# A decoder trunk's mixer: the tokens' factor folded into C and the convolved block, and some VectorE work pinned to a later place

## The chip, the cores and the metric

One core of a Trainium2 chip runs the whole program. The metric is the device time of one execution in microseconds (us); the times shown are medians of three runs. The profile comes from one further execution under the hardware profiler. Five engines work side by side, each in its own order: TensorE (PE, matmuls; PEld its weight loads), VectorE (DVE), ScalarE (ACT), GpSimd (POOL) and SyncE (SP). SP and GpSimd issue the transfers (DMAs) that are named here.

## The reference

Two layers of a decoder over 512 tokens of width 1024, everything float32. Each layer is a SwiGLU block, a mixer and another SwiGLU block. The mixer normalises, projects to q, k, v and three convolution parts, and joins attention and convolution by `w_out`:

```python
def short_conv(b_gate, c_gate, h_conv, conv_w):
    u = c_gate * h_conv
    ...
    y = lax.conv_general_dilated(
        u, w, window_strides=(1,), padding=[(CONV_K - 1, 0)],
        dimension_numbers=("NWC", "WIO", "NWC"), feature_group_count=CONV_WIDTH)
    return b_gate * y
...
        h = rms_norm(x, mix_norm[l])
        z = h @ w_in[l]
        ...
        attn_out = sliding_window_attention(q, k, v, attn_sink[l])
        conv_out = short_conv(z[..., V_END:CB_END], z[..., CB_END:CC_END],
                              z[..., CC_END:CH_END], conv_w[l])
        x = x + jnp.concatenate([attn_out, conv_out], axis=-1) @ w_out[l]
```

`rms_norm` divides each token by the root of its mean square and multiplies by a gain per feature. The convolution has three taps along the tokens and one filter for each of 512 features.

## The kernel before

Data lies transposed: features on the 128 partitions, the 512 tokens along the free axis. The norm's gain is put into the projection's input; the factor per token, `norm.inv` (the same value on all partitions, 128x512), is multiplied in after the matmul.

**Split numbers.** A float32 product is made of three matmuls in a rounded type: each matrix is split into a high part and the rest (`split`, L197: a copy on ScalarE, L198, and a subtraction on VectorE, L199). For weights the parts are the tiles `wh` and `wl`, three buffers of each. `split_far` (L201) makes the rest with a copy on ScalarE and an adding transfer that GpSimd issues (L205), and takes no VectorE time.

**Weights.** `plan` lists the 512 KB units in the order of use. `need_raw` gives a unit one of eight `raw` buffers and issues its load on SP (L182); a unit that is a sum of two blocks gets the second block by an adding transfer from GpSimd (L193). `need_split(g)` makes all splits up to number g, asking for loads LOAD_AHEAD = 4 units further. `take_split` (L257) hands out the split of the next matmul group, after `need_split` for SPLIT_AHEAD = 2 groups further.

**The mixer** (`mix`, L1149) of a layer has 18 groups of 24 matmuls (`group`, L263), each 128 columns of `w_in` by all tokens, into a PSUM tile `acc` (four buffers): k, v, four of q, and then for two pairs of feature blocks two of C, two of h and two of B. `scaled` (L1155) multiplies `acc` by `norm.inv` on VectorE into an SBUF tile: `cc`, `ch`, `cb`. From these: u = ch·cc (L1302, GpSimd), the three taps (L1304 and L1306 on ScalarE, L1307 on VectorE, L1310 on GpSimd) give y in the tile cc, and cb·y goes into `mixed[1]` (L1317, GpSimd; the last of the layer on VectorE).

Between these groups the attention runs in eight units (`Unit`), each with the stages `scores`, `turn` and `values`; `attend(step)` runs those that are due after the group of that step. `turn` transposes the probabilities p on TensorE into `pt` and splits them: `ph` on ScalarE, `pl` on VectorE (L1249). `values` then multiplies with the values into `o` (L1259 with ph, L1260 with pl).

**The output projection** uses a scheme with seven products of half-size blocks instead of eight (`Seven`, `share`). Its seven steps (`CHAINS`) multiply the blocks b11, b21, t2, t3, t1, t4, b22 of `mixed` (sums and differences of quarters) with the weights a11, a12, s2, s3, s1, a22, s4 of `w_out`, each weight in two halves h = 0 and 1. The accumulators are called x_m, w_m and y_m. s2 is the sum a11 + s1, made on VectorE in the raw buffers (L223). The blocks are split like weights: fb11h and fb11l, ft2h and ft2l and so on; t1, t4 and b22 are of the `far` kind. `soon` (L1323) says behind which step blocks are made early, in front of the additions into x (L747). Of a11, the first half is split by `split_far` in the `w_out` plan (L381).

**What sets the order.** A scheduler places the instructions of each engine when the program is built, by program order and by when it thinks their inputs ready; the waits of an engine are then in that fixed order. `tc.issue_after(ins)` adds one rule to it: what is recorded inside the block on the engine of `ins` comes behind `ins` on that engine. It adds no wait for `ins` to finish.

Of the kernel before, what the change touches and what calls it, by code (L numbers as in the profile page):

```python
# [1 line left out]

# [46 lines left out]
SPLIT_AHEAD = 2  # L49
# [9 lines left out]
def trunk_kernel(  # L59
# [23 lines left out]
    nc = tc.nc  # L83
# [11 lines left out]
    def g2(name, dt=F32, shape=(P, S)):  # L95
        return work.tile(list(shape), dt, tag="g2", bufs=14, name=name)
# [18 lines left out]
    def f32(ap):  # L115
        return ap.bitcast(F32)
# [50 lines left out]
    units = []  # L167
    order = []
    raw_of, split_of = {}, {}
    state = {"raw": 0, "split": 0, "group": 0}  # L170

    def add_unit(*unit):
        units.append(unit)
# [33 lines left out]
    def need_split(g):  # L207
        while state["split"] <= min(g, len(order) - 1):
            n = state["split"]
            u, what = order[n]  # L210
            far = what == "far"
            if what in (None, "wide", "far"):
                need_raw(u if far else u + LOAD_AHEAD)
                raw = raw_of.pop(u)
            elif isinstance(what, tuple):

                what, h, how = what
                far = how == "far"
                last = {"a11": 0, "a12": 4, "s2": 2, "s3": 6, "s1": 2, "a22": 8, "s4": 4}[what]
                need_raw(u + max(last, 4) + h + (0 if far else LOAD_AHEAD))  # L220
                a11, s1, a12, s3, a22 = (raw_of.get(u + 2 * i + h) for i in range(5))
                if what == "s2":
                    nc.vector.tensor_add(a11, a11, s1)  # L223
                raw = {"a11": a11, "a12": a12, "s2": a11, "s3": s3, "s1": s1, "a22": a22, "s4": a12}[what]
            else:

                need_raw(u + 4 + LOAD_AHEAD)
                a11, a12, s1, s3, a22 = (raw_of.get(u + i) for i in range(5))
                if what == "s2":
                    nc.vector.tensor_add(a11, a11, s1)  # L230
                if what == "s4":
                    nc.vector.tensor_add(a11, a11, a12)
                raw = {"a11": a11, "a12": a12, "s2": a11, "s3": s3, "s1": s1, "a22": a22, "s4": a11}[what]
                if what == FORMS[-1]:
                    for i in range(5):
                        del raw_of[u + i]
            shape = list(raw.shape)
            hi = wpool.tile(shape, F32R, tag="wh", bufs=3, name=f"wh_{n}")
            lo = wpool.tile(shape, F32R, tag="wl", bufs=3, name=f"wl_{n}")
            if far:  # L240
                split_far(hi, lo, raw)
            elif n:
                split(hi, lo, raw)
            if isinstance(order[n][1], tuple):
                if what == "s3" and how == "share":
                    nc.gpsimd.dma_start(out=a12, in_=a11, accum_op=ALU.add)
                elif what == "s3":
                    nc.vector.tensor_add(a12, a12, a11)
                done = {"s3": (0, 3), "s1": (1,), "a22": (4,), "s4": (2,)}.get(what, ())
                for i in done:  # L250
                    del raw_of[u + 2 * i + h]
            split_of[n] = (hi, lo)
            state["split"] += 1
            if far:
                need_raw(u + LOAD_AHEAD + (4 + h if isinstance(order[n][1], tuple) else 0))

    def take_split():  # L257
        n = state["group"]
        state["group"] += 1
        need_split(n + SPLIT_AHEAD if n else 0)  # L260
        return n, *split_of.pop(n)

    def group(rhs, between=None, own=None, order=range(KC)):  # L263
# [52 lines left out]
    def plan():  # L316
# [57 lines left out]
        for l in range(DEPTH):  # L374
            ffn(ffn1_wg[l], ffn1_wu[l], ffn1_wd[l], INNER if l else FIRST)
            for c in MIX_COLS:
                for j in range(2):
                    order.append((add_unit((w_in[l], 0, KC, (2 * c + j) * P, P)), None))
            seven(
                lambda o, j, h: (w_out[l], KC // 2 * j + 2 * h, 2, o * S, S),  # L380
                lambda what, h: "far" if (what, h) == ("a11", 0) else "share",  # L381
            )
            ffn(ffn2_wg[l], ffn2_wu[l], ffn2_wd[l], INNER if l + 1 < DEPTH else LAST)

# [168 lines left out]
    norm = Norm(0)  # L553
# [166 lines left out]
    def share(ops, by, between, y=None, soon=None):  # L720


        accs = {}
        for step, (acc, operand, start) in enumerate(CHAINS):
            ops.make(operand)
            xh, xl = ops.forms[operand]
            if start:
                tag = {"x": "mm", "y": "sc", "w": "aux"}[acc]
                shape = [P, 2, H] if y is None else [P, S]
                accs[acc] = [psum(tag, shape, f"{acc}_{ops.name}_{m}") for m in range(2)]  # L730
            o, t, sign = SHARES[step]
            for h in range(2):
                _, wh, wl = take_split()
                if y is None:
                    stand(accs[acc], wh, wl, xh, xl, h, start)
                else:
                    stream(accs[acc], wh, wl, xh, xl, h, start)
                if h == 0:
                    continue
                if soon:  # L740
                    ops.make(*soon.get(step, ()))
                for m in range(2):
                    if y is None:
                        part = xpair[2 * o + m][:, :, t * H : (t + 1) * H]
                    else:
                        part = y[2 * t + m][o]
                    nc.vector.scalar_tensor_tensor(  # L747
                        part, accs[acc][m], by * sign, part, op0=ALU.mult, op1=ALU.add
                    )
            if not soon and step < 3:  # L750
                ops.make(CHAINS[step + 4][1])
            between(step)
# [396 lines left out]
    def mix(l, norm, after):  # L1149
# [40 lines left out]
        class Unit:  # L1190
# [47 lines left out]
                    nc.vector.tensor_scalar(p, p, sums[:, h : h + 1], None, op0=ALU.mult)  # L1238

            def turn(self):  # L1240
                self.pt = []
                for kb in range(self.lo // P, 2):
                    tp = psum("aux", [P, 4, P], f"pt_{self.name}_{kb}")
                    for h in range(4):
                        nc.tensor.transpose(tp[:, h, :], self.p[:, h, kb * P : (kb + 1) * P], ident)
                    hi = g2(f"ph_{self.name}_{kb}", F32R, (P, 4, P))
                    lo = g2(f"pl_{self.name}_{kb}", F32R, (P, 4, P))
                    nc.scalar.copy(hi, tp)
                    nc.vector.tensor_sub(lo, tp, f32(hi))  # L1249
                    self.pt.append((kb, hi, lo))  # L1250

            def values(self):
                n, g = self.n, self.g
# [16 lines left out]

        def attend(step):

            for at, stage in ((VALUES_AT, "values"), (TURN_AT, "turn"), (SCORES_AT, "scores")):
                if step in at:
                    getattr(todo[at.index(step)], stage)()

        for j in range(NH // 2):
            acc = group(norm.h) if j else qacc
# [9 lines left out]
            q[2 * j], q[2 * j + 1] = qe, qo  # L1288
            attend(2 + j)

        step = 6
        for pair in range(2):
            cs = []
            for j in range(2):
                cs.append(scaled(group(norm.h), f"cc_{l}_{pair}_{j}"))
                attend(step)
                step += 1
            ys = []
            for j in range(2):
                c = 2 * pair + j  # L1300
                u = scaled(group(norm.h), f"ch_{l}_{pair}_{j}")
                nc.gpsimd.tensor_mul(u, u, cs[j])  # L1302
                y = cs[j]
                nc.scalar.activation(y, u, AF.Copy, scale=conv_of(l, 2, c))  # L1304
                tap = g2(f"tap_{l}_{c}")
                nc.scalar.activation(tap[:, 1:], u[:, : S - 1], AF.Copy, scale=conv_of(l, 1, c))  # L1306
                nc.vector.scalar_tensor_tensor(  # L1307
                    tap[:, 2:], u[:, : S - 2], conv_of(l, 0, c), tap[:, 2:], op0=ALU.mult, op1=ALU.add
                )
                nc.gpsimd.tensor_add(y[:, 1:], y[:, 1:], tap[:, 1:])  # L1310
                ys.append(y)
                attend(step)
                step += 1
            for j in range(2):
                b = scaled(group(norm.h), f"cb_{l}_{pair}_{j}")
                eng = nc.vector if pair and j else nc.gpsimd
                eng.tensor_mul(mixed[1][:, 2 * pair + j, :], b, ys[j])  # L1317
                attend(step)
                step += 1
                if step == 17:  # L1320
                    ops.make("b11")
        ops.make("b21", "b22")
        share(ops, 1.0, after.step, soon={0: ("t2", "t1"), 1: ("t3", "t4")})  # L1323

    class into:

# [53 lines left out]
```

## Time and profile before

| | us |
|---|---|
| median of three runs | 1692.35 (1691.88 to 1692.66) |
| the profiled execution's own time | 1690.47 |
| its span, first to last instruction | 1688.6 |
| mixer of layer one, first q group to the last `w_out` step | about 360 to 511 |
| the same in layer two | about 1194 to 1346 |
| granted TensorE clock, share of full | 0.999 |

The page of the profile gives each engine's busy time, then the chain of work that ended last, then groups of instructions by line. The waits view lists who waited for whom: total us, number of waits, the longest. The timeline gives start, duration, engine, line, operation, out<-in and shapes; the bracket behind a row is the idle time of the engine before it and who ended it. A 128x1024 operation of VectorE is listed with 1.22 us, but such operations follow each other at 1.14, since the end of one overlaps the start of the next. The same holds for 128x512 operations (0.69 listed, 0.60 apart) and for TensorE's matmuls (128x512: 0.39 listed, 0.23 apart; 128x256: 0.28 and 0.12).

### The profile page before, as it was taken

What the parts mean: (1) busy time and instruction counts of PE and PEld (TensorE: products, weight loads), DVE (VectorE), ACT (ScalarE), POOL (GpSimd) and SP (SyncE); (2) the same over time, 40 slices, a digit from 0 to 9 for tenths busy, and PEclk for the clock granted to TensorE, in tenths of its full rate; (3) what the DMA queues carried; (4) which work ended last, traced back from release to release, by engine and by line L of the source; (5) the groups of instructions that cost most, each with busy time, mean ns of one, the idle gap of its engine ahead of it and who ended that gap; (6) DMA issues with size and microseconds to landing.
All of it is one profiled execution on the core that took longest, in us unless ns stands there. A gap on an engine that the chain in (4) does not pass through costs nothing.

```text
span 1688.6 us, 23567 instructions
## 1 busy us (share of the span) xinstructions
PE 1675.1 (99%) x9014; PEld 1443.3 (85%) x9014; DVE 1382.8 (82%) x1817; ACT 967.7 (57%) x1335; POOL 215.3 (13%) x192
## 2 busy tenths in 40 slices
PE   9999999999999999999999999999999999999998
PEld 6888889988898888889988888999888988888886
DVE  7987679988799967799798677997787997667995
ACT  6545565466566655564465555644555766556654
POOL 1011111001221111111011111110013111111111
PEclk9999999999999999999999999999999999999999
DMA  8467787731597677778466777785226867777881
GB/s 250 104 171 189 186 199 187 188 100 51 135 215 167 174 183 186 187 191 221 150 144 179 187 186 183 198 202 156 63 63 143 219 137 195 184 183 185 224 213 51
DMA packets 191846, 284.19 MB, mean 168 GB/s; under 512 B 9004, under 2 KB 77684, under 8 KB 191732
## 3 DMA queue, kind: packets, MB, share of 16 engines
q1 hardware_dynamic: 151108, 199.95, 37.7%
q0 software_dynamic: 39472, 81.27, 28.6%
q8 instruction: 71, 1.16, 0.3%
q10 hardware_dynamic: 1152, 1.45, 0.2%
q14 instruction: 43, 0.35, 0.1%
HBM read 261.14 MB, written 2.10 MB: 156 GB/s over the span
## 4 chain that ended last, share of the span: by engine, by line
PE 93%; DVE 3%; DMA 2%; issue 1%; POOL 0%; ACT 0%; SPq 0%; ACTq 0%; POOLq 0%; DVEq 0%
PE x L711 25%; PE y L711 12%; PE x_s L696 8%; PE acc L273 7%; PE acc L276 7%; PE acc L280 7%; PE w L711 6%; PE y_s L696 4%; PE x_s L711 3%; PE w_s L696 2%; PE x_m L696 2%; PE at L917 2%; PE y_m L696 1%; PE y_s L711 1%; DMA wl<-raw 1%
## 5 line engine op out<-in xcount | busy, mean ns | idle before, releaser
L198 ACT CAST wh<-raw 128x1024 fp32r<-128x1024 f32 (+1 forms) x482 | 505.2, 1048 | 531.0 <-PE x L711 132.0
L199 DVE TENSOR_TENSOR wl<-raw,wh 128x1024 fp32r<-128x1024 f32 (+1 forms) x481 | 588.4, 1225 | 210.3 <-ACT wh L198 208.3
L273 PE MATMUL acc<-xh,wh 128*128 128x512 f32 x448 | 176.5, 394 | 0.1
L276 PE MATMUL acc<-xl,wh 128*128 128x512 f32 x448 | 175.5, 392 | 0.1
L280 PE MATMUL acc<-xh,wl 128*128 128x512 f32 x416 | 162.5, 391 | 0.0
L193 POOL DMA_DIRECT2D raw<-in_ffn_wu_dram x39 | 47.3, 1217 | 531.6 <-DMA raw<-in_ffn_wu_dram 306.8
L276 PEld LDWEIGHTS acc<-xl,wh 128*128 128x128 f32 x448 | 84.2, 188 | 18.5 <-DVE xl L421 1.7
L273 PEld LDWEIGHTS acc<-xh,wh 128*128 128x128 f32 x448 | 84.2, 188 | 17.1 <-issue 0.5
L280 PEld LDWEIGHTS acc<-xh,wl 128*128 128x128 f32 x416 | 78.1, 188 | 16.2
L193 POOL DMA_DIRECT2D raw<-in_ffn_wg_dram x39 | 47.2, 1249 | 228.0 <-DMA raw<-in_ffn_wu_dram 100.0
L223 DVE TENSOR_TENSOR raw<-raw,raw 128x1024 f32<-128x1024 f32 x58 | 70.9, 1229 | 6.3 <-DMA wl<-raw 5.7
L193 POOL DMA_DIRECT2D raw<-in_ffn_wd_dram x32 | 38.6, 1206 | 260.6 <-DMA raw<-in_ffn_wd_dram 142.4
L711 PE MATMUL w<-wh,fb21h 128*128 128x512 f32 x152 | 60.7, 399 | 0.0
L711 PE MATMUL x<-wh,ft2h 128*128 128x512 f32 x152 | 60.6, 398 | 0.0
L711 PE MATMUL y<-wh,ft3h 128*128 128x512 f32 x152 | 60.4, 398 | 0.0
L711 PE MATMUL w<-wl,fb21h 128*128 128x512 f32 x152 | 59.4, 391 | 0.0
L711 PE MATMUL x<-wl,ft2h 128*128 128x512 f32 x152 | 59.3, 390 | 0.0
L711 PE MATMUL y<-wh,ft3l 128*128 128x512 f32 x152 | 59.2, 390 | 0.0
L711 PE MATMUL y<-wl,ft3h 128*128 128x512 f32 x152 | 59.2, 390 | 0.0
L711 PE MATMUL w<-wh,fb21l 128*128 128x512 f32 x152 | 59.2, 389 | 0.0
L711 PE MATMUL x<-wl,fb11h 128*128 128x512 f32 x152 | 59.2, 389 | 0.0
L711 PE MATMUL x<-wh,fb11h 128*128 128x512 f32 x152 | 59.1, 389 | 0.0
(503 smaller groups left out, 4805.0 us busy)
## 6 DMA issues: line engine op xcount, KB each, us to landing
raw<-in_ffn_wu_dram SPq DMA_DIRECT2D x127, 512.0 KB, 4.3
raw<-in_ffn_wd_dram SPq DMA_DIRECT2D x104, 512.0 KB, 5.0
raw<-in_ffn_wg_dram SPq DMA_DIRECT2D x87, 512.0 KB, 5.0
raw<-in_ffn_wu_dram POOLq DMA_DIRECT2D x39, 512.0 KB, 8.0
raw<-in_ffn_wg_dram POOLq DMA_DIRECT2D x39, 512.0 KB, 6.0
raw<-in_w_in_dram SPq DMA_DIRECT2D x36, 512.0 KB, 3.6
raw<-in_ffn_wd_dram POOLq DMA_DIRECT2D x32, 512.0 KB, 8.4
raw<-raw POOLq DMA_DIRECT2D x20, 512.0 KB, 7.2
```

The source lines that it names most:

```text
L193: nc.gpsimd.dma_start(out=r, in_=rows_of(*more), accum_op=ALU.add)
L198: nc.scalar.copy(hi, raw)
L199: eng.tensor_sub(lo, raw, f32(hi))
L223: nc.vector.tensor_add(a11, a11, s1)
L273: nc.tensor.matmul(acc, hi[:, k, :], rhs[k][0], start=k == first, stop=False)
L276: nc.tensor.matmul(acc, hi[:, k, :], rhs[k][1], start=False, stop=n == 0 and k == last)
L280: nc.tensor.matmul(acc, lo[:, k, :], rhs[k][0], start=False, stop=k == last)
L696: nc.tensor.matmul(accs[c // 2][:, c % 2, :], w[:, k, cols], x_[:, 2 * h + k, :], start=start and c % 2 == 0 and h + k + i == 0, stop=h + ...
L711: nc.tensor.matmul(accs[u], x_[:, 2 * h + k, tok], w[:, k, :], start=start and h + k + i == 0, stop=h + k == 2 and i == 2, skip_group_chec ...
L917: nc.tensor.transpose(tp[:, t * P : (t + 1) * P], ups[t][:, c * P : (c + 1) * P], ident)
```

## The change

Four things change, all in the mixer and the helpers that it calls.

1. C is multiplied by the square of the token factor (`inv2`, made once per layer on GpSimd), straight from PSUM. h is multiplied from PSUM with that, which gives u without a tile of its own. y is multiplied by `norm.inv` on GpSimd. B is multiplied from PSUM with y, into `mixed`. The products of L1302 and L1317 on SBUF tiles go.
2. `product()` asks only for the splits one group ahead. The split of the second group ahead is made in `go_on`, after `attend`; where `attend` ran a `turn`, it is recorded behind that turn's last pl on the engine of that pl, VectorE.
3. The second half's sum of s2 (h = 1) is recorded behind the layer's last product on VectorE (`state["late"]`), and `soon` is read for each half of a step: t2 after the second half of step 0, t1 after the first half of step 1.
4. The first half of a11 of `w_out` is split as the others, no longer by `split_far`.

```diff
                 if what == "s2":
-                    nc.vector.tensor_add(a11, a11, s1)
+                    late = state["late"] if h else None
+                    with tc.issue_after(late) if late else nullcontext():
+                        nc.vector.tensor_add(a11, a11, s1)
...
-    def take_split():
+    def take_split(ahead=SPLIT_AHEAD):
         n = state["group"]
         state["group"] += 1
-        need_split(n + SPLIT_AHEAD if n else 0)
+        need_split(n + ahead if n else 0)
...
-                lambda what, h: "far" if (what, h) == ("a11", 0) else "share",
+                lambda what, h: "share",
...
+                if soon:
+                    ops.make(*soon.get((step, h), ()))
                 if h == 0:
                     continue
-                if soon:
-                    ops.make(*soon.get(step, ()))
...
-                    nc.vector.tensor_sub(lo, tp, f32(hi))
+                    last = nc.vector.tensor_sub(lo, tp, f32(hi))
...
+        inv2 = g2(f"inv2_{l}")
+        nc.gpsimd.tensor_mul(inv2, norm.inv, norm.inv)
         step = 6
+
+        def product():
+            return group(norm.h, own=take_split(SPLIT_AHEAD - 1))
+
+        def go_on():
+
+            nonlocal step
+            last = attend(step)
+            step += 1
+            with tc.issue_after(last.ins) if last else nullcontext():
+                need_split(state["group"] - 1 + SPLIT_AHEAD)
...
-                cs.append(scaled(group(norm.h), f"cc_{l}_{pair}_{j}"))
+                c = g2(f"cc_{l}_{pair}_{j}")
+                nc.vector.tensor_mul(c, product(), inv2)
+                cs.append(c)
...
-                u = scaled(group(norm.h), f"ch_{l}_{pair}_{j}")
-                nc.gpsimd.tensor_mul(u, u, cs[j])
+                u = g2(f"ch_{l}_{pair}_{j}")
+                nc.vector.tensor_mul(u, product(), cs[j])
...
+                nc.gpsimd.tensor_mul(y, y, norm.inv)
...
-                b = scaled(group(norm.h), f"cb_{l}_{pair}_{j}")
-                eng = nc.vector if pair and j else nc.gpsimd
-                eng.tensor_mul(mixed[1][:, 2 * pair + j, :], b, ys[j])
+                last = nc.vector.tensor_mul(mixed[1][:, 2 * pair + j, :], product(), ys[j])
+                go_on()
...
+        state["late"] = last.ins
         ops.make("b21", "b22")
-        share(ops, 1.0, after.step, soon={0: ("t2", "t1"), 1: ("t3", "t4")})
+        share(ops, 1.0, after.step, soon={(0, 1): ("t2",), (1, 0): ("t1",), (1, 1): ("t3", "t4")})
+        state["late"] = None
```

More of the change, by code (lines that the diff above doesn't have):

```diff
@@ L1 @@
-from contextlib import ExitStack
+from contextlib import ExitStack, nullcontext
 import concourse.bass as bass
@@ L169, in trunk_kernel @@
     raw_of, split_of = {}, {}
-    state = {"raw": 0, "split": 0, "group": 0}
+    state = {"raw": 0, "split": 0, "group": 0, "late": None}
     def add_unit(*unit):
@@ L1248, in turn @@
                     nc.scalar.copy(hi, tp)
-                    nc.vector.tensor_sub(lo, tp, f32(hi))
+                    last = nc.vector.tensor_sub(lo, tp, f32(hi))
                     self.pt.append((kb, hi, lo))
+                return last
             def values(self):
@@ L1271, in attend @@
         def attend(step):
+            done = None
             for at, stage in ((VALUES_AT, "values"), (TURN_AT, "turn"), (SCORES_AT, "scores")):
                 if step in at:
-                    getattr(todo[at.index(step)], stage)()
+                    done = getattr(todo[at.index(step)], stage)() or done
+            return done
         for j in range(NH // 2):
@@ L1294, in mix @@
             for j in range(2):
-                cs.append(scaled(group(norm.h), f"cc_{l}_{pair}_{j}"))
-                attend(step)
-                step += 1
+                c = g2(f"cc_{l}_{pair}_{j}")
+                nc.vector.tensor_mul(c, product(), inv2)
+                cs.append(c)
+                go_on()
             ys = []
@@ L1310, in mix @@
                 nc.gpsimd.tensor_add(y[:, 1:], y[:, 1:], tap[:, 1:])
+                nc.gpsimd.tensor_mul(y, y, norm.inv)
                 ys.append(y)
-                attend(step)
-                step += 1
+                go_on()
             for j in range(2):
-                b = scaled(group(norm.h), f"cb_{l}_{pair}_{j}")
-                eng = nc.vector if pair and j else nc.gpsimd
-                eng.tensor_mul(mixed[1][:, 2 * pair + j, :], b, ys[j])
-                attend(step)
-                step += 1
+                last = nc.vector.tensor_mul(mixed[1][:, 2 * pair + j, :], product(), ys[j])
+                go_on()
                 if step == 17:
                     ops.make("b11")
+        state["late"] = last.ins
         ops.make("b21", "b22")
-        share(ops, 1.0, after.step, soon={0: ("t2", "t1"), 1: ("t3", "t4")})
+        share(ops, 1.0, after.step, soon={(0, 1): ("t2",), (1, 0): ("t1",), (1, 1): ("t3", "t4")})
+        state["late"] = None
     class into:
```

## The prediction

> **What bounds the kernel now.** I read the busy table and the chain of waits first, then TensorE's own waits, then the timelines of the mixer (360 to 511 us in the first layer, 1194 to 1346 in the second).
>
> ```profile
> PE 1675.1 (99%) x9014; PEld 1443.3 (85%) x9014; DVE 1382.8 (82%) x1817; ACT 967.7 (57%) x1335; POOL 215.3 (13%) x192
> ...
> PE 93%; DVE 3%; DMA 2%; issue 1%; POOL 0%; ACT 0%; SPq 0%; ACTq 0%; POOLq 0%; DVEq 0%
> ```
>
> TensorE is nearly always busy and the edit takes no matmul away. So only TensorE's waits can be won, and these are few:
>
> ```profile
> PE o L1260 <- DVE pl L1249: 1.2, 2, 0.6
> PE x_m L696 <- DVE wl L199: 0.9, 2, 0.5
> ...
> PE w_m L696 <- DVE fb21l_m L199: 0.5, 1, 0.5
> ```
>
> Those are all the waits of the mixer that this view names. Idle time understates them, because a modelled matmul end covers part of the gap. TensorE's timeline gives them from start to start (columns: start, duration, engine, line, what; in brackets the idle time and who ended it):
>
> ```profile
> 456.27 0.39 PE L1259 MATMUL o<-ph,vv 128*128 128x512 f32 x1
> 457.24 0.51 PE L1260 MATMUL o<-pl,vv 128*128 128x512 f32 x1 [0.59 <-DVE pl L1249]
> ...
> 482.13 0.28 PE L696 MATMUL x_m<-ft2l_m,wh 128*128 128x256 f32 x1
> 482.83 0.39 PE L696 MATMUL x_m<-ft2h_m,wl 128*128 128x256 f32 x1 [0.41 <-DVE wl L199]
> 483.05 0.28 PE L696 MATMUL x_m<-ft2h_m,wh 128*128 128x256 f32 x1
> ```
>
> The first pair is 0.97 apart where such matmuls follow at 0.23: 0.74 lost. The second is 0.70 where 0.12 is usual, and the next start is 0.10 late: 0.68 lost. In the second layer the same places are 1290.02 (0.74) and 1316.63 to 1317.64 (0.77), and a third is 1309.77 to 1310.76 at w_m (0.75). Sum: 1.42 in layer one, 2.26 in layer two, **3.68 us in all**.
>
> VectorE's timeline shows why:
>
> ```profile
> 453.92 0.68 DVE L1249 TENSOR_TENSOR pl<-pt,ph 128x512 fp32r<-128x512 f32 x1
> 454.75 1.84 DVE L199 TENSOR_TENSOR wl<-raw,wh 128x1024 fp32r<-128x1024 f32 x1
> 456.51 0.68 DVE L1249 TENSOR_TENSOR pl<-pt,ph 128x512 fp32r<-128x512 f32 x1
> ...
> 465.90 1.23 DVE L223 TENSOR_TENSOR raw<-raw,raw 128x1024 f32<-128x1024 f32 x1 [2.45 <-DMA wl<-raw]
> ...
> 471.02 0.68 DVE L1158 TENSOR_TENSOR cb<-acc,inv 128x512 f32<-128x512 f32 x1
> 471.80 0.69 DVE L1317 TENSOR_TENSOR m<-cb,cc 128x512 f32<-128x512 f32 x1
> ...
> 481.56 2.35 DVE L199 TENSOR_TENSOR wl<-raw,wh 128x1024 fp32r<-128x1024 f32 x2
> ```
>
> A look-ahead split (wl) stands between the two pl that TensorE needs. Later, from 465.90 on, VectorE runs without a gap and reaches the split of s2 at 481.56, when TensorE is already there.
>
> **Part 1, the folded factor.** Per layer the eight products lose these: on GpSimd four multiplies of L1302 (1.29) and three of L1317 (1.30 to 2.13), on VectorE one L1317 (0.69). They gain on GpSimd one inv² and four y·inv; the nearest row is L1302, the same two-operand 128x512 multiply, 1.29 each. So GpSimd goes from 7 to 5 such multiplies. The product read from PSUM (acc with cc instead of inv) has L1158's form: 0.69, unchanged. Off TensorE this costs nothing; what it buys is that the last product is in `mixed` 0.6 after its matmul ends, not at 472.4. The y·inv multiply lies in front of cb: y2's add follows tap at 453.6, so y2 is ready by about 456.3 and cb wants it at 463.2; y3 is ready by 462.9 and wanted at 469.5. If that cover went, each us late would be a us on the last product.
>
> GpSimd also slows VectorE: the wl at 454.75 takes 1.84, not 1.22, beside the add that GpSimd runs from 454.09 to 455.49. Seven such overlaps become five; I count no gain for it.
>
> **Part 2, splits behind the pl.** In the built program VectorE's order becomes pl, pl, wl. The second pl then ends at about 454.8 instead of 457.2, and TensorE wants it at 456.3 (456.27 plus one pitch, less the 0.15 of part 4): gain 0.74 in each layer. The price is that each split comes one product later. What waits behind it is the next group's third matmul. The tightest is the last product's: its split starts after the last turn's pl, at 461.2 to 462.3, or at 462.9 if GpSimd's y3 multiply goes first, and ends at 462.4 to 464.05; TensorE wants it at 464.35. The SP loads that wait for a split also move (most wait for `DVE wl` now); they take 3.6 to 4 us to land, except 7.2 for one at 458.65 beside GpSimd transfers. The tightest, that of a12's second half, would land by 465.9 and is copied at 472.4. GpSimd's four w_out accumulations now queue behind y·inv: the second is issued at about 456.3 not 452.95, lands 6.3 later at 462.6 to 464, and its sum is taken at 470.2. All hidden.
>
> **Part 3, a11's first split leaves the transfer.** Removed: an ACT copy (1.05), a GpSimd issue (0.90) and its transfer, for which VectorE stood still 2.45 (3.28 in layer two). Added: one VectorE subtraction of 1.14 (pitch of the wl rows). It fits in that idle stretch: nothing on the path.
>
> **Part 4, s2's second sum and t1 pinned.** Four transposes (pt) also move out of the middle of a product to between o and sc. The in-and-out at 398.13 to 399.90 costs 0.35 over the pitch, the entry behind an o (457.24 to 457.58) 0.11 and the first sc behind transposes (421.09) 0.08: gain 0.15 a layer.
>
> Now the chain behind the last product. TensorE is 0.74 + 0.15 earlier, so that product is free at 470.45 − 0.89 = 469.55. VectorE then has, in its new order up to the split of s3's first half: thirteen 128x1024 operations (s2 sum, two a12 splits, fb21l, three for t3, t2 and t4, t1, ft2l, ft3l, two s2 splits, s3's) at the 1.14 pitch = 14.8, and five PSUM-fed 128x512 at 0.60 = 3.0. End: 487.4. On the way, w_m's fb21l is done at 473.6 (wanted 475.2), ft2l at 480.4 (wanted 481.0), s2's splits at 479.4 and 482.8 (wanted 481.1 and 483.8), ft3l at 486.2 (wanted 486.8). So the waits at x_m and, in layer two, w_m go: gains 0.68, and 0.77 + 0.75. But TensorE, whose first projection matmul comes at 470.26 − 0.89 = 469.37 and whose steps last 5.76 (476.01 to 481.77), wants s3's split with the fifth matmul of step 3, at 469.37 + 3·5.76 + 0.48 = 487.1, and gets it at 487.4 plus 0.14 (as at 482.69 to 482.83): **a new wait of 0.4, with restart 0.5, at y_m**, each layer. The trace before has no such wait; its bounds are 0 (if VectorE's chain is 0.4 shorter) and 1.7 (one operation of 1.14 more in front of it: 0.4 + 1.14 + 0.1). I take 0.5, from the pitch rows of the same stretch.
>
> t1 moves from 478.09 to about 480.5, so ft1l's transfer, issued at 481.46 before and landed at 488.69, is issued at about 483.0 and lands at 490.3; TensorE wants it at 492.9. Cover 2.6.
>
> [...]
>
> **Sum.** Layer one 0.74 + 0.68 + 0.15 − 0.5 = 1.07; layer two 0.74 + 0.77 + 0.75 + 0.15 − 0.5 = 1.91; together 3.0. The profiled execution had span 1688.6 and took 1690.47: after, 1687.5. The median shown, 1692.35, is 1.88 above that execution; on its scale **1689.4**.
>
> **Rivals.** One: the chain at y_m keeps up (VectorE's overlaps with GpSimd fall from seven to five, against: those lie before 469). Then the 1.0 of new waits is not paid: 1688.4. [...] Three, slower: the look-ahead cut from two products to one makes TensorE wait for wl at the head of a product wherever a turn stands before it, eight a layer. It decides as soon as pl runs more than the cover later than reckoned (0.3 to 1.6 us at the five tightest). At 1.3 (one GpSimd multiply) late and 0.8 of cover, 0.5 + 0.1 restart × 16 = 9.6: 1699. For: the split is pinned behind transposes, copy and pl, each on another engine; against: before six of the twelve products of layer one VectorE stands idle, 0.26 to 1.66. [...] That the pins do nothing is excluded: VectorE's built order differs.
>
> **How the numbers follow.** Forecast 0.46 (its own range 1688.9 to 1690.5), one 0.21, two 0.15, three 0.14, four 0.04. 0.2% is 3.4 us, about what a measurement tells from no change: the line lies at 1688.97. Faster takes rival one and a little of the forecast's range, 0.23; slower is rival three, 0.14; the rest 0.63. The range, 1687.8 to 1692.9, holds all but three and some spread beyond one.
>
> **What would show it.** Right: no wait of o for pl; none of w_m for fb21l, none of x_m for wl; a wait of y_m for wl of some 0.4 in each layer; VectorE gapless from about 469.6 to 487. Wrong: a wait of acc for wl (rival three), of x_m for ft1l (four), or y_m without a wait (one).

## The result and the profile after

The changed kernel took 1687.42 us (median of 10 runs, 1686.32 to 1688.55), the kernel before 1691.51 in the 10 runs beside it. The ratio is 0.9971 (95% interval 0.9963 to 0.9979). The forecast was 1689.4 with a range down to 1687.8, so the gain was larger than forecast (4.1 between these two medians, 3.0 forecast) and the time lies just under the range.

The page of the changed kernel, busy table and chain of waits:

```profile
PE 1674.2 (99%) x9014; PEld 1444.2 (86%) x9014; DVE 1380.9 (82%) x1817; ACT 965.5 (57%) x1333; POOL 207.6 (12%) x186
...
PE 96%; DVE 3%; issue 0%; ACT 0%; ACTq 0%; DVEq 0%
```

TensorE's busy time is what it was (1675.1 before); its share of the chain went from 93% to 96%, and DMA has left the chain. TensorE's own waits (us in total, times, longest):

```profile
PE acc L275 <- DVE x L992: 1.9, 3, 0.7
PE idle L125 <- DVE warm L580: 1.2, 1, 1.2
PE y_m L698 <- DVE wl L199: 0.5, 2, 0.2
PE acc L275 <- ACT xh L422: 0.2, 1, 0.2
```

The waits of o, x_m and w_m are gone; of the mixer only y_m is named, and it is new. TensorE's timeline at the two places (start, duration, engine, line, what):

```profile
456.15 0.39 PE L1263 MATMUL o<-ph,vv 128*128 128x512 f32 x1
456.38 0.39 PE L1264 MATMUL o<-pl,vv 128*128 128x512 f32 x1
456.61 1.03 PE L1248 MATMUL pt<-ident,p 128*128 128x128 f32 x8
...
486.92 0.28 PE L698 MATMUL y_m<-ft3l_m,wh 128*128 128x256 f32 x1
487.44 0.39 PE L698 MATMUL y_m<-ft3h_m,wl 128*128 128x256 f32 x1 [0.25 <-DVE wl L199]
487.67 0.28 PE L698 MATMUL y_m<-ft3h_m,wh 128*128 128x256 f32 x1
```

The second o by pl follows at the pitch of 0.23, and so does the first transpose behind it: before, these two distances were 0.97 and 0.34. At y_m, 0.52 stands where 0.12 is usual and the next start comes 0.11 late (what is lost at the start just behind a wait is called restart here): 0.51, as forecast. VectorE's timeline around the last product:

```profile
466.39 1.23 DVE L199 TENSOR_TENSOR wl<-raw,wh 128x1024 fp32r<-128x1024 f32 x1
469.55 0.69 DVE L1337 TENSOR_TENSOR m<-acc,cc 128x512 f32<-128x512 f32 x1 [1.94 <-PE acc L282]
470.16 1.22 DVE L225 TENSOR_TENSOR raw<-raw,raw 128x1024 f32<-128x1024 f32 x1
...
485.04 1.21 DVE L199 TENSOR_TENSOR ft3l_m<-sums_m,ft3h_m 128x1024 fp32r<-128x1024 f32 x1
486.18 2.35 DVE L199 TENSOR_TENSOR wl<-raw,wh 128x1024 fp32r<-128x1024 f32 x2
```

The product is taken at 469.55 and s3's first split ends at 487.3 (486.18 plus a pitch of 1.14), to 0.1 what the forecast's chain gave. But look at the first two lines: VectorE stands idle for 1.94 in front of the product, and the raw sum behind it needs nothing of the product.

Read from start to start at the same matmuls of both traces (negative is gained; in brackets the forecast):

| stretch | layer one | layer two |
|---|---|---|
| conv and attention products, up to the first projection matmul | -1.19 (-0.89) | -1.23 (-0.89) |
| w_m | 0 (0) | -0.74 (-0.75) |
| x_m | -0.67 (-0.68) | -0.77 (-0.77) |
| y_m | +0.50 (+0.5) | +0.50 (+0.5) |

The sum is -3.6; the other stages lose 0.2 again, most of it at the first load. The spans say 1685.2 against 1688.6.

### The profile page after: what moved, and what is told of

Same layout as the page of the kernel before. It is cut to its first block, busy times and chain, and to the rows that moved or that the text cites. A ratio compares the mean times of both kernels' runs of the same rounds, so it can differ in the third digit from the quotient of the medians.

```text
span 1685.2 us, 23535 instructions
## 1 busy us (share of the span) xinstructions
PE 1674.2 (99%) x9014; PEld 1444.2 (86%) x9014; DVE 1380.9 (82%) x1817; ACT 965.5 (57%) x1333; POOL 207.6 (12%) x186
## 4 chain that ended last, share of the span: by engine, by line
PE 96%; DVE 3%; issue 0%; ACT 0%; ACTq 0%; DVEq 0%
PE x L713 25%; PE y L713 12%; PE x_s L698 8%; PE acc L275 8%; PE acc L278 8%; PE acc L282 7%; PE w L713 6%; PE y_s L698 4%; PE x_s L713 3%; PE w_s L698 2%; PE at L919 2%; PE x_m L698 1%; PE y_m L698 1%; PE y_s L713 1%; PE pt L1248 1%; PE x L833 1%
```

## The experiments

Theory: the gain is TensorE's waits, which VectorE's order set, and each part of the change acts through what stands on VectorE around the last product. Rivals: each part brings its own share; or GpSimd's multiplies are the cause; or the gain lies outside the mixer.

**One part at a time, from the kernel before.** The fold alone (its products as in the change, the rest as before):

```diff
...
-                u = scaled(group(norm.h), f"ch_{l}_{pair}_{j}")
-                nc.gpsimd.tensor_mul(u, u, cs[j])
+                u = g2(f"ch_{l}_{pair}_{j}")
+                nc.vector.tensor_mul(u, group(norm.h), cs[j])
...
+                nc.gpsimd.tensor_mul(y, y, norm.inv)
...
+                nc.vector.tensor_mul(mixed[1][:, 2 * pair + j, :], group(norm.h), ys[j])
...
```

> The kernel before with the folded factor alone (no splits behind the pl, a11's first half by its transfer, no pins). Theory (VectorE's order sets TensorE's waits): TensorE's work up to the last product stays as it was, so the wait of o for pl stays (0.74, with restart 0.85, in each layer) and so do the transposes. Behind the last product VectorE has one operation of 0.69 less: s2's split ends at about 482.0 where TensorE wants it at 482.0, fb21l at 473.9 (wanted 476.1), s3's split at 487.7 (wanted 488.0). So the waits at x_m (0.68 and 0.77) and w_m (0.75) go and none comes: span 2.2 shorter than before's 1688.6, some 1686.4. Rival (the fold is worth nothing by itself, as the prediction had it; its sums need the pins as well): span within 0.5 of before. Rival (GpSimd's fewer multiplies speed VectorE up in all of the mixer): the o wait shrinks too, span more than 3 shorter.

Measured: span 1686.1, median 1688.64, ratio 0.9983 (0.9975 to 0.9992). Its waits of TensorE:

```profile
PE acc L273 <- DVE x L990: 1.9, 3, 0.7
PE o L1260 <- DVE pl L1249: 1.4, 2, 0.8
...
```

No w_m, no x_m, and the o wait still there, somewhat longer. From start to start, x_m gains 0.67 in layer one, w_m and x_m 0.74 and 0.77 in layer two. So the fold by itself takes all that the forecast had summed at x_m and w_m with the four parts together. Two things differ in this trace, and the run doesn't separate them: VectorE has one operation less behind the last product, and GpSimd, without the multiply of ch by cc, issues a11's transfer at 457.67 instead of 459.09, so that the first raw sum begins at 464.5 instead of 465.90.

The splits behind the pl alone (shown at C; h and B likewise):

```diff
-                cs.append(scaled(group(norm.h), f"cc_{l}_{pair}_{j}"))
-                attend(step)
-                step += 1
+                cs.append(scaled(product(), f"cc_{l}_{pair}_{j}"))
+                go_on()
```

> The kernel before with the look-ahead splits behind the pl alone (no fold, a11's first half by its transfer, no pins of s2 and t1). Theory: TensorE gains 0.85 at o and some 0.36 at the transposes in each layer, but VectorE's raw sum of w_out now waits for the transfer of a11's first half, which is issued a product later and lands at about 469.5 to 470; both raw sums stand ahead of the last product, fb21l ends at 476.8 instead of 475.8 and s2's split at 483.7 instead of 482.7, while TensorE comes 1.2 sooner. So what is gained before x_m is lost at w_m and x_m: span 0 to 2 longer than before's 1688.6. Rival (each part's gain stands alone): the span is 2.4 shorter, with no larger wait at w_m or x_m.

Measured: span 1690.6, median 1691.87, ratio 0.9998 (0.9989 to 1.0007). Its waits of TensorE, those of the mixer and one of a feed-forward stage:

```profile
PE x L711 <- DMA wl<-raw: 1.5, 1, 1.5
...
PE w_m L696 <- DVE fb21l_m L199: 1.0, 2, 0.5
PE x_m L696 <- DVE wl L199: 1.0, 2, 0.5
PE pt L1245 <- DVE p L1238: 0.9, 2, 0.5
```

o no longer waits, but w_m now does in both layers, and the transposes of 2_0 (1_0 and 2_0 are two of the attention's units) wait 0.62 for p, 0.46 more than before. VectorE's sum, on which p hangs, shows why; before it took 0.37:

```profile
405.66 1.17 DVE L1234 TENSOR_TENSOR sums<-sums,es 128x4 f32<-128x4 f32 x1 [0.29 <-ACT es L1233]
```

It now begins just behind GpSimd's multiply of ch by cc (405.52, for 1.29), more of which below. In the mixer 0.2 is left of the gain; the 1.5 is a transfer of a feed-forward stage. The theory holds in part. As it said, a11's transfer lands a product later (the first raw sum begins at 469.4) and the chain behind takes back what is won: in layer one 0.47 is won ahead of x_m and 0.86 lost at w_m and x_m. In layer two, where w_m waited before too, the 0.55 won stays. The wait for p, half of what the splits win at o, was not expected.

a11's first half split by VectorE, alone:

```diff
-                lambda what, h: "far" if (what, h) == ("a11", 0) else "share",
+                lambda what, h: "share",
```

> The kernel before with one thing changed: a11's first half is split by VectorE and not by its transfer (no fold, no splits behind the pl, no pins). Theory: VectorE's raw sums no longer wait for a transfer (2.45 and 3.28 of idle before), both are done ahead of the last product, cb is taken at 470.5 instead of 471.02, fb21l is done in time in both layers and s2's split at 482.2 (wanted 482.25): the waits at w_m (0.75 in layer two) and x_m (0.68, 0.77) fall to 0.2 in all, o's stays; span 1.9 shorter than before's 1688.6, some 1686.7. The time gains more than the span, since the transfer's landing scatters: median 2 to 3.5 below before's. Rival (the prediction's reading: nothing on the path): span and time within 0.5.

Measured: span 1686.9, median 1689.12, ratio 0.9985 (0.9976 to 0.9994). The raw sums are done by 468.6, and VectorE waits for the product:

```profile
470.69 0.69 DVE L1158 TENSOR_TENSOR cb<-acc,inv 128x512 f32<-128x512 f32 x1 [2.06 <-PE acc L280]
```

From start to start x_m gains 0.55 in layer one, w_m and x_m 0.74 and 0.64 in layer two. A part that the forecast costed at nothing takes the same waits as the fold, all but 0.1 at x_m in each layer: either makes VectorE's chain early enough, so the two don't add up.

**One part undone, from the changed kernel.** a11's split by its transfer again (the line above, turned round):

> The changed kernel with one thing undone: a11's first half is split by its transfer again. The prediction costed that part at nothing on the path. Theory: with the splits one product later the transfer lands at about 470 and s2's first raw sum, which stands ahead of the last product on VectorE, waits for it; the chain behind the last product starts some 1.6 later than 469.55, and y_m's wait for the split of s3 grows from 0.5 to about 2.1 in each layer: span 3.2 longer than the changed kernel's 1685.2, some 1688.4. Rival (the prediction's reading): no difference over 0.3 in the span. Bound from below: if the transfer lands before 468.6, no difference.

Measured: span 1686.2, median 1688.08, ratio 0.9979 (0.9970 to 0.9988). VectorE's timeline there:

```profile
468.39 1.23 DVE L225 TENSOR_TENSOR raw<-raw,raw 128x1024 f32<-128x1024 f32 x1 [2.44 <-DMA wl<-raw]
469.53 0.68 DVE L1337 TENSOR_TENSOR m<-acc,cc 128x512 f32<-128x512 f32 x1
```

My expectation failed: the transfer landed at 468.4, not at 470, and its sum was just done when the product was (cover 0). In the mixer the span is 0.2 longer; the other 0.8 is x waiting for a transfer in a feed-forward stage. Beside the rest of the change this part is worth next to nothing in this execution, with no margin.

The fold undone (the first diff, turned round, with product() for group):

> The changed kernel with the fold alone undone (three GpSimd multiplies of a product more in each layer, one VectorE operation more behind the last product; splits behind the pl, a11's first half split by VectorE, both pins kept). Theory: the second turn's transposes wait some 0.6 for p, as in the kernel with the splits alone (0.46 more than before); the last product is in mixed 0.7 to 0.8 later, VectorE reaches the split of s2's second half at about 485.7 where TensorE wants it at 483.7 plus that 0.6 to 0.7, so x_m waits some 1.5 to 2 in place of y_m's 0.5: 1.6 to 2.3 a layer, span 3 to 4.6 longer than the changed kernel's 1685.2. Rival (the prediction's reading, the fold buys only that the last product is 0.6 sooner, and GpSimd's multiplies cost nothing): y_m waits 0.7 longer and nothing else moves, span 1.4 longer.

Measured: span 1690.7, median 1692.52, ratio 1.0003 (0.9994 to 1.0012). In the two layers the products lose 0.6 and 1.0, x_m 1.85 and 1.86, and y_m gains its 0.5 in each: 4.3 lost in the two layers together, in the upper half of what was expected (another 1.0 is a feed-forward transfer). In the products it is mostly GpSimd's multiply again (the sum takes 1.15, and the transposes wait 0.62 for p). At x_m it is a new order: without the fold the scheduler put s2's second sum at 481.78, where the changed kernel has it at 470.16, and x_m waits for the copy (0.46 of idle) and for the split (0.88) made from it. So the rest of the change is worth nothing without the fold, but the run shows the fold together with the place of that sum, not the fold by itself.

s2's second sum not pinned:

```diff
-        state["late"] = last.ins
```

> The changed kernel without the pin of s2's second raw sum behind the last product. Theory: VectorE works without a gap from there to s3's split either way, so the sum only changes its place in the chain, fb21l ends at about the same time (473.6) and y_m's wait stays 0.4 to 0.6: span within 0.3 of the changed kernel's 1685.2 (waits of single transfers in the feed-forward stages left out). Rival (the pin is what takes the wait from w_m and x_m): w_m waits for fb21l some 0.7 in the second layer, or x_m for wl, span 0.7 to 2 longer.

Measured: span 1684.1, median 1685.97 (6 runs), ratio 0.9967 (0.9955 to 0.9979). Both expectations failed: y_m's wait is gone in both layers (0.50 gained in each, from start to start). VectorE's timeline:

```profile
467.49 1.23 DVE L225 TENSOR_TENSOR raw<-raw,raw 128x1024 f32<-128x1024 f32 x1
469.40 0.69 DVE L1337 TENSOR_TENSOR m<-acc,cc 128x512 f32<-128x512 f32 x1 [0.68 <-PE acc L282]
...
485.01 1.22 DVE L199 TENSOR_TENSOR wl<-raw,wh 128x1024 fp32r<-128x1024 f32 x1
```

The sum has gone back into the idle stretch ahead of the product, and s3's split begins at 485.01 where it began at 486.18. The pin had carried 1.14 of work out of free time into a full chain. The expectation looked only at the chain from the product on, which has no gap; the 1.94 of idle stands in front of the product, and there the sum costs nothing.

t1 after step 0 again:

```diff
-        ... soon={(0, 1): ("t2",), (1, 0): ("t1",), (1, 1): ("t3", "t4")})
+        ... soon={(0, 1): ("t2", "t1"), (1, 1): ("t3", "t4")})
```

> The changed kernel with t1 made after step 0 again, s2's second sum still pinned. Theory (behind the last product VectorE's chain is full, and t1's place only decides who waits): s2's split ends at 481.6 where TensorE wants it at 481.3, so x_m waits 0.5 with its restart; s3's split is then in time, y_m's wait goes; span within 0.2 of the changed kernel's 1685.2. Rival (t1's place carries the gain at x_m and costs nothing): x_m waits 0.5 and y_m still waits 0.5, span 1.0 longer.

Measured: span 1685.5, median 1687.27, ratio 0.9974 (0.9963 to 0.9984). x_m loses 0.53 and y_m gains 0.50 in each layer, as the theory had it: behind a full chain t1's place only chooses who waits. (0.7 of a feed-forward transfer and 0.5 less at the first load stand in this span.)

Both pins off, that is the two edits above together:

> The changed kernel without either pin: s2's second sum where the scheduler puts it (before the last product, in VectorE's idle time) and t1 after step 0; the fold, the splits behind the pl and a11's split by VectorE kept. Theory: with the sum out of the chain VectorE reaches s2's split at 480.4 (wanted 481.1) and s3's at 486.2 (wanted 487.0), so no projection matmul waits in either layer: span 1684.1, as without the first pin alone, 1.1 shorter than the changed kernel's, ratio 0.9968 within 0.0012. Rival (t1 has to be late): x_m waits for wl in both layers, span 1685 or more.

Measured: span 1684.3, median 1686.24 (5 runs), ratio 0.9967 (0.9955 to 0.9980); no projection matmul waits. t1 needs no delay once the sum is out of the chain. t4 half a step later, with the pins kept, takes the same wait another way:

```diff
-        ... (1, 1): ("t3", "t4")})
+        ... (1, 1): ("t3",), (2, 0): ("t4",)})
```

> The changed kernel with t4 made half a step later, so that one operation of 1.14 less stands ahead of the split of s3 on VectorE. Theory (y_m's new wait of 0.5 is VectorE's chain and nothing else): s3's split ends at about 486.2 or sooner, TensorE wants it at 487.0, the wait of y_m for wl goes in both layers, ft3l (486.2) is still 0.6 ahead of its use, and t4's transfer lands ahead of its step: span 1.0 shorter than the changed kernel's, some 1684.2. Rival (the wait moves to ft3l or to t4's transfer): y_m for ft3l or a later step for ft4l waits 0.3 to 1 instead, span within 0.3 or longer.

Measured: span 1684.4, median 1687.26 (7 runs), ratio 0.9970 (0.9959 to 0.9981); y_m gains 0.50 in each layer. These three (the first pin off, both off, t4 later) beat both kernels by the span; over the changed kernel the 0.8 to 1.1 is seen in the traces and is within the intervals of the times.

The early splits as before, only those of the second half of the products behind the pl:

```diff
-            return group(norm.h, own=take_split(SPLIT_AHEAD - 1))
+            return group(norm.h, own=take_split(SPLIT_AHEAD - (step >= 12)))
...
+            if step < 13:
+                return
             with tc.issue_after(last.ins) if last else nullcontext():
```

> The changed kernel with the splits put behind the pl only in the second half of the products, so that the turns of units 1_0 and 2_0 stand as before. Theory: the o wait stays away; the transposes of 1_0 go back into the middle of a product and wait 0.17 for p again, with two entries and exits of 0.09 more, those of 2_0 stay without a wait since that one is GpSimd's multiply and the fold took it: 0.27 a layer, span 0.5 longer than the changed kernel's 1685.2. Rival (the transposes' whole 0.35 a layer comes from the splits' place): 0.7 longer. Rival (it is o alone): no difference.

Measured: span 1685.6, median 1687.93, ratio 0.9976 (0.9967 to 0.9985). The span is 0.4 longer. The transposes of 1_0 wait 0.17 for p again, as in the kernel before; those of 2_0 do not. That is the theory's picture, but the products lose 0.11 and 0.16 in the two layers, half of its 0.27 a layer; 0.1 of the span lies elsewhere.

**GpSimd against VectorE.** Before, the first transpose of 2_0 began 0.39 after the matmul ahead of it (407.72 to 408.11), 0.16 over the pitch, and the view of waits names nothing there. One multiply moved, in the kernel before:

```diff
-                nc.gpsimd.tensor_mul(u, u, cs[j])
+                (nc.gpsimd if c else nc.vector).tensor_mul(u, u, cs[j])
```

> The kernel before with one thing changed: the multiply of ch by cc of the first convolution channel runs on VectorE, which is idle there for 0.69, instead of on GpSimd. The order of everything else stays as built. Theory (GpSimd's multiply holds up VectorE's 128x4 sum, and with it p): the sum takes 0.15 to 0.17 and not 0.37, p is scaled 0.3 to 0.5 sooner, and the transposes of unit 2_0 follow their matmul by 0.23 to 0.25 instead of 0.39 (0.16 less, in each layer); the o wait, which is set by VectorE, grows by the same 0.16, so the span stays within 0.3 of before's. Rival (the 0.16 is the cost of turning TensorE to transposes): the distance stays at 0.39.

Measured: span 1689.2, median 1691.51, ratio 0.9998 (0.9989 to 1.0007). VectorE's line of the sum in the kernel before (0.37, while GpSimd multiplies from 405.51 for 1.29) and then in this one:

```profile
406.46 0.37 DVE L1234 TENSOR_TENSOR sums<-sums,es 128x4 f32<-128x4 f32 x1
```

```profile
406.60 0.16 DVE L1234 TENSOR_TENSOR sums<-sums,es 128x4 f32<-128x4 f32 x1
```

The transposes then follow at 0.22 (407.86 to 408.08; in layer two at 0.23, where it was 0.39). So the 0.16 was a wait for p, caused by GpSimd, that a modelled matmul end had covered. The o wait did not grow as I expected; the span is 0.5 longer by a wait of w_m in layer one, told under the scatter. The reverse, one multiply more in the changed kernel, whose result nobody reads:

```diff
                 nc.vector.tensor_mul(u, product(), cs[j])
+                if c == 0:
+                    spare = const.tile([P, S], mybir.dt.bfloat16, tag="spare", name=f"spare_{l}")
+                    nc.gpsimd.tensor_mul(spare, u, cs[j])
```

> The changed kernel with one GpSimd multiply of the first convolution channel added in each layer, into a tile that nothing reads, at the place where the kernel before multiplied ch by cc. Nothing waits for its result. Theory (VectorE's two-operand work does not get on while GpSimd multiplies, and TensorE pays for it): the 128x4 sum of 0.15 at 405.7 takes up to 1.2, p is scaled 0.4 to 0.6 later, the transposes of unit 2_0 wait 0.3 to 0.6 for p: span 0.6 to 1.2 longer than the changed kernel's. Rival (GpSimd is off the path): the sum stays at 0.17 and the span within 0.2.

Measured: span 1694.1, median 1695.22, ratio 1.0018 (1.0009 to 1.0027): 4.4 lost in each layer, far more than expected. VectorE's and then GpSimd's timeline:

```profile
405.56 1.07 DVE L1236 TENSOR_TENSOR sums<-sums,es 128x4 f32<-128x4 f32 x1 [0.32 <-ACT es L1235]
...
407.68 3.26 DVE L1240 TENSOR_SCALAR p<-p,sums 128x256 f32<-128x256 f32 x4
```

```profile
405.32 1.28 POOL L1327 TENSOR_TENSOR spare<-ch,cc 128x512 bf16<-128x512 f32 x1 [42.65 <-DVE ch L1324]
407.93 1.26 POOL L1335 TENSOR_TENSOR cc<-cc,tap 128x511 f32<-128x511 f32 x1 [1.32 <-DVE tap L1332]
409.27 1.26 POOL L1336 TENSOR_TENSOR cc<-cc,inv 128x512 f32<-128x512 f32 x1
```

The sum, 0.17 in the changed kernel, takes 1.07 and ends with GpSimd's multiply. That part was expected. The edit also made the scheduler put tap ahead of p, so GpSimd's next add and multiply ran beside the four scalings of p, which took 3.26 and not 1.14; TensorE waited three times inside the transposes. So this kernel shows VectorE's work stretched beside GpSimd's, but not what one multiply costs by itself. The kernel with the splits alone comes nearer: there one multiply stretches the sum to 1.17, and the transposes wait 0.62 in place of 0.16.

**The scatter.** Before's profiled execution was faster than all ten of its timed runs. Every timed run has a span too, and its time is that span plus 1.7 to 1.9. Of the 93 runs of the kernel before that were timed beside the experiments none has a span under the profiled 1688.6; the medians of their four sets are 1690.0 to 1690.4. The changed kernel's median span is 1685.6 in its ten runs, 0.4 above the profiled 1685.2. The changed kernel and the kernel before were run again, unaltered:

> The changed kernel once more, unaltered, for the scatter. Expected: span 1685.2 within 0.3, but for a single wait of a feed-forward stage for a transfer (0 to 1.8 in the runs so far), the same y_m wait of 0.5 in each layer, and a ratio to before within 0.9963 to 0.9985. Were the gain of 4.1 between the medians, 0.7 more than the spans', a property of the kernel and not of the runs, the ratio would come out at 0.9976 or below again; from the spans alone it would be 0.998.

Measured: span 1685.1, median 1687.41, ratio 0.9975 (0.9964 to 0.9985), the y_m wait as before. The ratio alone doesn't tell 0.9976 from 0.998. The spans tell more: the median of these eight is 1685.6 again, 4.4 under the 1690.0 of the kernel before beside them, where the two profiled executions are 3.4 apart. So the part of the gain that is not in the two traces compared above belongs to the kernels, and not to those ten runs.

> The kernel before once more, unaltered, to see how far the landing of a11's transfer moves between executions. Theory (the execution shown of before had a landing that cost w_m nothing in layer one, others have not): VectorE's first raw sum starts at 465.9 to 468 in layer one; for each us past 465.9 w_m waits that much in layer one (1.03 where the sum came at 466.9), and the span is that much longer. Rival (the extra 0.7 to 1.5 of before's median come from other stages): the sum starts at 465.9 and w_m does not wait in layer one, though the span is over 1689.3.

> As for the run before it: the kernel before, unaltered, once more. Theory: span minus 1688.6 equals the w_m wait of layer one plus what x (in a feed-forward stage) waits for a transfer and what the first load costs at the start. Rival: it does not.

> As for the two runs before it: the kernel before, unaltered, once more. Theory: span minus 1688.6 equals the w_m wait of layer one plus what x (in a feed-forward stage) waits for a transfer and what the first load costs at the start. Rival: it does not.

Measured: spans 1689.3, 1688.8 and 1689.7. VectorE's first raw sum of layer one in the three, in this order:

```profile
466.58 1.23 DVE L223 TENSOR_TENSOR raw<-raw,raw 128x1024 f32<-128x1024 f32 x1 [3.35 <-DMA wl<-raw]
```

```profile
466.15 1.23 DVE L223 TENSOR_TENSOR raw<-raw,raw 128x1024 f32<-128x1024 f32 x1 [2.52 <-DMA wl<-raw]
```

```profile
466.83 1.22 DVE L223 TENSOR_TENSOR raw<-raw,raw 128x1024 f32<-128x1024 f32 x1 [3.27 <-DMA wl<-raw]
```

In layer one w_m then waits 0.80, 0 and 0.72; in the execution of the prediction (465.90) it was 0, in the kernel with one multiply moved (466.9) 1.03. The landing of one transfer moved by up to 1 us between these five executions, and TensorE paid for it in layer one in three of them. What counts is how long before the first projection matmul the sum begins. In the two layers of these five executions this lead and the wait of w_m add up to 4.27 to 4.29 wherever w_m waits (from a lead of 3.26 with a wait of 1.03 to 3.81 with 0.47); at 4.29 and 4.36 it doesn't wait. So the 0.75 of layer two in the forecast's sum is the same wait, and it was 0.47 to 0.74 in these executions. The span's excess over 1688.6 is made of this, of the first load (-0.4 to +0.2) and of small steps of 0.1 to 0.3 elsewhere, so the theory holds for its main term and not as an equation.

## Why the prediction was right and wrong

Against 1689.4 the miss is 1.98. It splits into 1.44 of scale (the forecast added 1.88 to the profiled execution's scale; the changed kernel's median lies 0.44 above its own) and 0.5 of terms (1687.5 forecast on that scale, 1686.98 taken).

- **The step that failed most: "the median shown, 1692.35, is 1.88 above that execution; on its scale 1689.4".** The 1.88 was carried over as a constant. It is span, and it belongs to the kernel before: its median spans lie 1.4 to 1.8 above the execution that the forecast read, the changed kernel's 0.4. The execution read was a short one. Part of what the longer ones have is wait, of the kind that the change removes: in the three repeats the mixer took 1.1, 0.0 and 0.6 more than in the execution summed, most of it w_m's in layer one, where the sum had 0. Another 0.1 to 0.8 is that the three shown runs lie above the later medians (1691.51; in the later sets 1691.8 to 1692.2). The rest stays open, since no trace kept of the kernel before is as long as its median (the longest has 1689.7); single waits of a feed-forward stage for a transfer (0.7 to 1.8 in four of the kernels) are a candidate that was not tested.
- **Part 3, "nothing on the path"**: wrong for the kernel before, where it is worth 1.7 of span and 3.1 of median alone; beside the other parts it is right, within the 0.2 of the one execution without it.
- **Part 1, "I count no gain for it"** of the overlaps with GpSimd: one of the seven held p back, 0.16 a layer. And the fold, costed at nothing but an earlier last product, alone takes x_m and w_m.
- **Part 2**: right, the o wait goes, no split came late (rival three did not occur). Mis-sized: 0.74 where 0.85 was lost. The 0.11 of restart was booked as the price of turning to transposes ("457.24 to 457.58") and charged at 1_0 too; in the changed kernel that turn costs nothing (456.38 to 456.61). These two 0.11 and the 0.16 of GpSimd account, within 0.1, for the 0.3 a layer by which the products gained more than summed.
- **Part 4**: the transposes of 1_0 moved as read from the build; their 0.35 was in part a wait for p of 0.17, since a split stood ahead of nm on VectorE. The y_m wait came with its 0.5. That it is the pin's own doing was not seen: "gapless from about 469.6" was looked at, the idle 1.94 before it was not. "That the pins do nothing is excluded" is true, but what they do is a loss: without them the span is 0.9 shorter.
- The waits at x_m and w_m went as summed, to 0.01. ft1l's issue took 1.28 again (483.22; 481.46 in the kernel before), and x_m has no wait for ft1l, so what the forecast numbers four did not come.

## What to carry to other kernels

Before pinning an operation behind another, see whether it stood in idle time: a pin that moves free work into a full chain sells one wait for another. Parts that feed one chain don't add: cost each both alone and beside the others. A transfer that just fits in one profiled execution can be a wait in others (here w_m waited 0 in the execution of the prediction and 0.80, 0 and 0.72 in three more), so compare the profiled execution's span with those of the timed runs, and several executions with each other, before a difference between median and profile is carried over as a constant.

## What the runs showed of the hardware

In the kernel with one multiply more, VectorE's operations took longer beside GpSimd's. The sum on 4 columns took 1.07 instead of 0.17: it began at 405.56, while GpSimd multiplied from 405.32 to 406.60, and ended at 406.63. The four scalings of 256 columns took 3.26 instead of 1.14, from 407.68 to 410.94, while GpSimd added and multiplied from 407.93 to 410.53. The other way round, in the changed kernel GpSimd's multiply at 454.52 took 2.17 instead of 1.29 beside VectorE's split, which ran until 455.53.

TensorE's granted clock was lower behind a row of waits. In the kernel with one multiply more, by windows (us, PE busy, PEld busy, DVE busy, ACT busy, POOL busy, PEclk, DMA share, GB/s):

```profile
409.00:411.90 2.90, 1.60 (x9) 1.17 (x10) 2.87 (x6) 0.48 (x1) 1.45 (x2) 0.98 0.00 0
411.90:415.10 3.20, 3.20 (x9) 2.51 (x8) 3.20 (x9) 0.59 (x2) 0.00 (x0) 0.50 0.02 5
415.10:418.00 2.90, 2.90 (x14) 2.38 (x13) 1.01 (x5) 0.87 (x1) 0.00 (x0) 0.99 0.47 138
```

After three waits of 0.41, 0.93 and 0.90 the granted clock was 0.50 over the 3.20 us of the second row. Eight matmuls, 411.92 to 414.90, came at 0.43 there instead of 0.23: 1.6 on top of the waits. Over the whole execution the clock was 0.997, against 0.999 in the changed kernel. TensorE was not idle ahead of it: in the first row it was busy for 1.60 of 2.90. Nor does that share tell when the clock falls: with the fold undone TensorE was busy for 1.66 of 3.00 at the wait of x_m (484.00 to 487.00), and the clock was 1.00 in that window and in the one behind it. What took it down in the one kernel and not in the other, no run here shows.
